# First modulation in blocks of 256 columns, query scores one tile on, and the norms' first roots and second chain in another order

## The chip, the cores and the metric

The kernel runs on one core of a Trainium2 chip. The metric is the device time of one execution in microseconds (us), the median of several runs. A core has TensorE (PE in the rows; its weight loads are PEld), VectorE (DVE), ScalarE (ACT), GpSimd (POOL) and SyncE (SP, which here issues most of the transfers). Each works through a queue of its own in order and waits for the others by semaphores.

## The reference, cut to what is computed

A trunk of two layers over 256 tokens of 1024 columns, in fp32. Layer 0 mixes the tokens with differential attention and a spatial gate, layer 1 with a multi-scale pool; after each mixer stands a PEER layer (product keys, 16 of 16384 experts for each of 8 heads).

```python
for i in range(DEPTH):
    sh1, sc1, g1, sh2, sc2, g2 = jnp.split((silu_c @ ada_w[i] + ada_b[i])[:, None, :], 6, axis=-1)
    hx = modulate(xs, sh1, sc1)                      # xs * (1 + sc1) + sh1
    if ctx_out or even:
        csh1, csc1, cg1, csh2, csc2, cg2 = jnp.split(silu_cc @ ada_w[i] + ada_b[i], 6, axis=-1)
        hc = modulate(cs, csh1, csc1)                # the context, layer 0 alone
    ...
        yx, yc = mixer_ab(hx, hc, ab_w_in[j], ...)   # even; the first product is (hx @ w_in)
    ...
        yx = mixer_pool(hx, pool_w_in[j], ...)       # odd
    xs = layer_norm(alpha * xs + g1 * yx, ln_g[i, 0], ln_b[i, 0])
    hx = modulate(xs, sh2, sc2)
    ...
    fx = peer(hx.reshape(-1, d), peer_wq[i], peer_keys[i], peer_u[i], peer_v[i])
    xs = layer_norm(alpha * xs + g2 * fx, ln_g[i, 1], ln_b[i, 1])
```

What the change touches are the first `modulate` (shift and scale come from 2048 columns of `ada_w[0]`, for the tokens and for the context), the `layer_norm` ahead of each `peer`, the one between the two layers, and the beginning of `peer`: the queries (`hx @ wq`), their scores against the keys, and the search for the best 16.

## The kernel before, in words

**Weights.** All large weights come as tiles of 128 x 1024, in the order in which they are used. A list of items is written out by hand and run in order; every engine's queue holds what the code issues, in that order. For each tile ScalarE copies a rounded high half `hi` (L64), and VectorE, or in the PEER stages GpSimd, makes the low half `lo` by subtraction (L68). A product is three products of halves: high by high, high by low, low by high. `ahead` splits tiles up to three ahead of their use.

**Around a tile.** `item(src, run, after)` is a tile, its products and what is done behind them. `defer(f)` puts `f` off until the products of the next item are issued; nested, it puts it off by as many tiles. `work(budget)` issues a share of the background steps in `bg` (VectorE's searches for the best 16, and the routing that follows) behind each tile. What stands behind a waiting instruction on the same queue waits too.

**Start.** Sixteen adaptive tiles (eight for the shift, eight for the scale) are multiplied by the silu of the two conditions into rows of two partitions (products at L156 to L158, `adrow` copied at L545), turned into columns (L562), added to the bias (L563), and the scale is incremented (L550). `modulated(q)` then makes four blocks of 256 tokens of the input in the two halves: ScalarE with an activation for the high half (L582), VectorE (for `q` of 0) or GpSimd with a multiplication (L584), VectorE the low half by subtraction (L585); `q` of 2 and 3 is the context. The first four tiles of `w_in` are the gate's (`natural`, L610), the next four the gate's input (`transposed`, L616), followed by others and by attention.

**Norms.** Tokens stand in two blocks of 128. `half(nb, c)` is called as each half (512 columns) of a block's output is summed; `norm_part` adds the residual and makes the statistics (up to the variance, L236), `norm_end(nb)` the reciprocal root (L180 to L196, small VectorE instructions; `n_nm` at L251) and the normalised block (L254 on ScalarE, L256 on VectorE), `to_hT` transposes it (L273), scales it (L278, L281) and makes the two halves (L285, L287, L290; the put-off low halves at L943). `mixed` does so ahead of PEER, `second_start` between the layers. In the latter the next stage's first three weight tiles are multiplied block by block: `rowsum_product(..., early=True)` issues 18 products for the first block, in the order of parts 0, 2, 1 (high by high, high of h by low of w, low of h by high of w), and `settle_block` the second block's transposes.

**PEER.** Behind two tiles of keys and 16 tiles of `wq` come 128 tiles of `uT`. Two tiles make one head's query (`query`, L161 and L162), `score` its scores (L156 to L158, copied at L1005), and the searches go into `bg` (L1013 on). `routed` puts the softmax of the routing and the decoding in; the routing's results are transposed at L1093 and L1097. Products with `h` are L984, L985 and L988.

```python
        self.norm_part(nb, c)
        if (nb, c) == (1, 0):
            for _ in self.norm_end(0):
                pass
...
                if j % 2:
                    h = j // 2
                    query(h, st["p"])
                    self.defer(lambda: self.defer(lambda: score(h)))
```

## Time and profile before

| | |
|---|---|
| runs | 2037.8, 2038.82, 2040.18 us |
| median | 2038.82 us |
| profiled execution | 2038.5 us, of which the span is 2036.7 us |
| mean granted clock of TensorE | 0.986 of full speed |
| TensorE busy | 1965.6 us (97%) |
| VectorE busy | 1558.0 us (76%) |
| ScalarE busy | 969.6 us (48%) |
| GpSimd busy | 289.9 us (14%) |
| transfers | 389.93 MB, mean 191 GB/s |

The times of an engine's busy work are sums over the span; what an engine waits for is read from the views of waits and of the timeline. In a timeline each row has its start and its duration in us, the engine, the line of the kernel, the operation, output and inputs by name, and the count of instructions that the row sums; in brackets at its end the idle time before it and what ended that. A matmul's row is longer than its share of the pipeline, since the next starts before it ends: the distance between starts is what it costs.

### The profile page before, as it was taken

Reading aid. Unit: us, or ns where it says so; the run is one execution under the profiler, and the core shown is the slowest. Engines: PE = TensorE matmul, PEld = TensorE weight load, DVE = VectorE, ACT = ScalarE, POOL = GpSimd, SP = SyncE. Lnnn points to the kernel's source line nnn. Section 1 sums busy time; section 2 is a strip of 40 time slices with the busy share of each in tenths; the row PEclk is TensorE's granted clock in tenths of the full one; section 3 lists DMA queues with packets and bytes.
Section 4 is the critical chain, followed back from the end, with each engine's and each line's share of the span. In section 5 each row is a group of like instructions: output and inputs, shape, how many; then the busy total and the mean of one; then the engine's idle time right before and its main releaser. Section 6 shows DMA issues by size and latency. Waiting matters only on the chain.

```text
span 2036.7 us, 34041 instructions
## 1 busy us (share of the span) xinstructions
PE 1965.6 (97%) x13348; PEld 1771.4 (87%) x13348; DVE 1558.0 (76%) x2775; ACT 969.6 (48%) x1354; POOL 289.9 (14%) x134
## 2 busy tenths in 40 slices
PE   8899989999999999999999889999999999999997
PEld 4889869999999998888778779999999998888886
DVE  6878878998888757777776679998888655555566
ACT  6444554544544444444445554445544444444442
POOL 0100007891000000000000016890000000000001
PEclk9899999999999999999999989999999999999999
DMA  8534335554444558888877445554444556555663
GB/s 305 216 135 159 132 116 174 177 176 165 157 148 150 170 185 285 291 305 293 288 263 223 144 161 161 182 176 165 156 146 147 177 180 198 191 195 195 219 236 113
DMA packets 108178, 389.93 MB, mean 191 GB/s; under 512 B 12777, under 2 KB 12905, under 8 KB 108017
## 3 DMA queue, kind: packets, MB, share of 16 engines
q1 hardware_dynamic: 105416, 382.28, 55.8%
q10 hardware_dynamic: 2024, 3.38, 0.5%
q8 instruction: 104, 1.70, 0.3%
q0 software_dynamic: 576, 2.10, 0.3%
q14 instruction: 58, 0.47, 0.1%
HBM read 384.55 MB, written 3.16 MB: 190 GB/s over the span
## 4 chain that ended last, share of the span: by engine, by line
PE 66%; DVE 25%; ACT 4%; issue 3%; DMA 2%; ACTq 0%; SPq 0%; DVEq 0%
PE pa L323 26%; PE px L323 8%; PE pa L984 8%; PE pa L985 7%; PE pa L988 7%; PE pt L1136 2%; DVE lo L68 2%; ACT hi L64 2%; PE pa L616 1%; DVE oh L1063 1%; DVE oh L1068 1%; DVE topi L1014 1%; DVE sc L1015 1%; DVE topi L1017 1%; PE pa L870 1%
## 5 line engine op out<-in xcount | busy, mean ns | idle before, releaser
L64 ACT ACTIVATE hi<-raw 128x1024 fp32r<-128x1024 f32 x599 | 632.6, 1059 | 581.5 <-PE px L323 357.0
L68 DVE TENSOR_TENSOR lo<-raw,hi 128x1024 fp32r<-128x1024 f32 x491 | 599.5, 1224 | 368.8 <-ACT hi L64 366.8
L984 PE MATMUL pa<-h,hi 128*128 128x256 f32 x2304 | 577.9, 288 | 1.5 <-DVE h L287 1.3
L985 PE MATMUL pa<-h,hi 128*128 128x256 f32 x2304 | 566.2, 283 | 0.3
L323 PE MATMUL pa<-hi,h 128*128 128x512 f32 x1524 | 471.7, 391 | 3.3 <-ACT h L285 1.6
L984 PEld LDWEIGHTS pa<-h,hi 128*128 128x128 f32 x2304 | 441.8, 192 | 2.5 <-DVE h L287 2.1
L985 PEld LDWEIGHTS pa<-h,hi 128*128 128x128 f32 x2304 | 442.6, 192 | 0.9 <-DVE h L290 0.9
L323 PEld LDWEIGHTS pa<-hi,h 128*128 128x128 f32 x1524 | 286.3, 188 | 65.9 <-ACT h L285 1.8
L988 PE MATMUL pa<-h,lo 128*128 128x256 f32 x2304 | 323.4, 283 | 0.0
L988 PEld LDWEIGHTS pa<-h,lo 128*128 128x128 f32 x2304 | 297.7, 192 | 0.0
L68 POOL TENSOR_TENSOR lo<-raw,hi 128x1024 fp32r<-128x1024 f32 x106 | 271.0, 2575 | 81.9 <-ACT hi L64 81.6
L323 PE MATMUL pa<-lo,h 128*128 128x512 f32 x762 | 256.5, 391 | 0.1
L323 PE MATMUL px<-hi,h 128*128 128x512 f32 x508 | 197.5, 389 | 0.0
L323 PEld LDWEIGHTS pa<-lo,h 128*128 128x128 f32 x762 | 143.8, 189 | 30.6 <-DVE lo L68 0.5
L1150 ACT ACTIVATE A<-pt 128x256 f32<-128x256 f32 (+31 forms) x182 | 50.9, 310 | 229.1 <-DVE A L1148 215.9
L949 POOL DMA_DIRECT2D xhd<-xh x4 | 2.4, 596 | 960.0 <-PE pt L273 949.8
L323 PEld LDWEIGHTS px<-hi,h 128*128 128x128 f32 x508 | 95.3, 188 | 19.8
L1127 DVE TENSOR_TENSOR m<-e,gd 128x512 f16<-128x512 f16 x256 | 105.4, 454 | 2.2
L323 PE MATMUL px<-lo,h 128*128 128x512 f32 x254 | 98.8, 389 | 0.0
L259 POOL TENSOR_TENSOR aw<-aw 128x512 f32<-128x512 f32 x4 | 5.3, 1344 | 644.6 <-ACT aw L254 644.4
L393 DVE SCALAR_TENSOR_TENSOR aacc<-aw,csil,aacc 128x1024 f32<-128x1024 f32 x70 | 89.5, 1279 | 3.5 <-DMA aw<-in_ada_w 3.4
L1136 PE MATMUL pt<-m,e 128*128 128x128 f16 x1024 | 81.7, 220 | 3.2 <-DVE m L1127 1.0
(365 smaller groups left out, 2151.7 us busy)
## 6 DMA issues: line engine op xcount, KB each, us to landing
raw<-in_uT SPq DMA_DIRECT2D x256, 512.0 KB, 3.5
raw<-in_peer_v SPq DMA_DIRECT2D x256, 512.0 KB, 4.1
aw<-in_ada_w SPq DMA_DIRECT2D x80, 512.0 KB, 5.3
raw<-in_w_in SPq DMA_DIRECT2D x32, 512.0 KB, 4.1
raw<-in_wq SPq DMA_DIRECT2D x32, 512.0 KB, 3.8
raw<-in_ab_w_out SPq DMA_DIRECT2D x12, 512.0 KB, 3.5
raw<-in_ada_w SPq DMA_DIRECT2D x8, 512.0 KB, 5.9
xraw<-in_ada_w SPq DMA_DIRECT2D x8, 512.0 KB
```

Source lines behind the costliest of these rows:

```text
L64: nc.scalar.activation(hi, it["raw"], AF.Copy)
L68: low()
L323: nc.tensor.matmul(acc[2 * nb + a // 512], s[x], w[:, a:b], start=i == 0 and part == 0, stop=i == last and part == 2)
L393: nc.vector.scalar_tensor_tensor(st["acc"], w, c, st["acc"], op0=OP.mult, op1=OP.add)
L616: nc.tensor.matmul(o, (hi, lo)[x][:, 128 * k:128 * k + 128], f(k)[y], start=k == 0 and part == 0, stop=k == 7 and part == 2)
L870: nc.tensor.matmul(p, h(k, s)[x], tiles[k // 4][y][:, 256 * (k % 4):256 * (k % 4) + 256], start=part == 0 and k == 0, stop=part == 2 and k ...
L984: mm(out, hi[:, cs], hh, start=k == 0, stop=False)
L985: mm(out, hi[:, cs], hl, start=False, stop=False)
L988: mm(out, lo[:, cs], self.h(k)[0], start=False, stop=k == 7)
L1127: nc.vector.tensor_tensor(v4(x), v4(st["e1"][:, s]), wide(st["gd"][i], ch, 4), op=OP.mult)
L1136: nc.tensor.matmul(p[:, 128 * j:128 * j + 128], e2[:, j], m[i][:, j], start=i == 0, stop=i == 1)
L1150: nc.scalar.activation(x[:, e:], y[:, e:], AF.Copy, scale=1.0 / 4096)
```

## The change

**Start.** The adaptive columns are laid out anew on the host (`ada01`): four quarters of four tiles, each tile holding two row blocks of 256 shift and 256 scale columns. `quarter(c)` multiplies one quarter's four tiles, copies a row of 512, and, one or two tiles later, turns it into columns and modulates two blocks of 256 tokens. The quarters 1, 2 and 3 stand between the gate tiles in the list of items. The multiplications for the tokens are all VectorE's now (into a tile `xmod`). The context's modulation, `modulated_ctx`, has both its activations on ScalarE; before, GpSimd made the multiplications for three of the four input halves. The context is loaded behind the fourth gate tile in place of the second. **Norms.** `norm_end(0)` stands behind the first block's second half, (0, 1), in place of the second block's first half, (1, 0), in both norms. Between the layers the first block's low halves (`rest`) stand behind the second block's `norm_end`, and `settle_block` stands ahead of part 1 of the first block's products, so behind 12 of the 18. **Query.** `score(h)` is put off by one more tile, and `routed` is called after `uT` tile 2 in place of 1.

```diff
@@ -332,9 +332,10 @@
                     tail.append(x)
                     if i == EARLY - 1:
                         for part in (0, 2, 1):
+                            if part == 1:
+                                self.settle_block()
                             for x in tail:
                                 product(*x, 0, parts=(part,))
-                        self.settle_block()
                         for part in (0, 2, 1):
                             for x in tail:
                                 product(*x, 1, parts=(part,))
@@ -530,59 +531,66 @@
         self.hook(start)
-        for j in range(2):
...
-        def columns_of(j, row):
+        def quarter(c):
+            for kk in range(4):
+                def run(hi, lo, kk=kk):
+                    if kk == 0:
+                        st["ad"] = self.px() if c % 2 else self.pa()
+                    for i in range(2):
+                        k, cs = 2 * kk + i, slice(512 * i, 512 * i + 512)
+                        self.mm3(st["ad"][0:2], (self.cparts[0][:, k], self.cparts[1][:, k]), (hi[:, cs], lo[:, cs]), k == 0, k == 7)
+                    if kk < 3:
+                        return
+                    row = st["G"].tile([2, 512], FT, name="adrow", bufs=2)
+                    nc.scalar.activation(row, st["ad"][0:2], AF.Copy)
+
+                    def turned():
+                        columns_of(c, row)
+                        modulated(c)
+                    if c == 3:
+                        self.defer(turned)
+                    else:
+                        self.defer(lambda: self.defer(turned))
+                self.item(a["ada01"][c, kk], run, after=(lambda: inputs(0, [c])) if kk == 1 and c < 2 else None,
+                          own=(lambda: st["E"]) if kk % 2 else None, owned=2, early=kk % 2)
+
+        def columns_of(c, row):
             p = self.pt()
-            for b in range(8):
+            for b in range(4):
                 nc.tensor.transpose(p[:, 2 * b:2 * b + 2], row[:, 128 * b:128 * b + 128], self.ident[0:2, 0:2])
-            nc.vector.tensor_add(st["cc"][:, j], p[:, :16].rearrange("p (k o) -> p k o", o=2),
-                                 self.adabc[:, 0, j][:, :, None].to_broadcast([128, 8, 2]))
-
-
-        self.holds += 1
+            ks = slice(2 * c, 2 * c + 2)
+            for j in range(2):
+                nc.vector.tensor_add(st["cc"][:, j, ks], p[:, 4 * j:4 * j + 4].rearrange("p (k o) -> p k o", o=2),
+                                     self.adabc[:, 0, j, ks][:, :, None].to_broadcast([128, 2, 2]))
+            nc.vector.tensor_scalar(st["cc"][:, 1, ks], st["cc"][:, 1, ks], 1.0, None, op0=OP.add)
...
-        def modulated(q):
-            if q == 0:
+        def modulated(c):
+            if c == 0:
                 self.hhi, self.hlo = self.htiles()
-            x, y = st["in"][q], st["in"][q | 2]
-            hi = self.hhi[q] if q < 2 else st["hc"][q - 2]
-            lo = self.hlo[q] if q < 2 else st["hc"][q]
-            for k in range(4):
-                kk, o = 4 * (q % 2) + k, q // 2
-                sc, sh = st["cc"][:, 1, kk, o:o + 1], st["cc"][:, 0, kk, o:o + 1]
-                nc.scalar.activation(hi[:, k], x[:, k], AF.Identity, scale=sc, bias=sh)
-                eng = nc.gpsimd if q else nc.vector
-                eng.tensor_scalar(y[:, k], x[:, k], sc, sh, op0=OP.mult, op1=OP.add)
-            nc.vector.tensor_sub(lo, y, hi.bitcast(FT))
+            q, ks = c // 2, slice(2 * (c % 2), 2 * (c % 2) + 2)
+            x, hi, lo = st["in"][q], self.hhi[q], self.hlo[q]
+            y = st["G"].tile([128, 2, 256], FT, name="xmod", bufs=1)
+            for k in range(2):
+                i, kk = 2 * (c % 2) + k, 2 * c + k
+                sc, sh = st["cc"][:, 1, kk, 0:1], st["cc"][:, 0, kk, 0:1]
+                nc.scalar.activation(hi[:, i], x[:, i], AF.Identity, scale=sc, bias=sh)
+                nc.vector.tensor_scalar(y[:, k], x[:, i], sc, sh, op0=OP.mult, op1=OP.add)
+            nc.vector.tensor_sub(lo[:, ks], y, hi[:, ks].bitcast(FT))
+        def modulated_ctx(q):
+            x, hi, lo = st["in"][2 + q], st["hc"][q], st["hc"][2 + q]
+            for i in range(4):
+                kk = 4 * q + i
+                sc, sh = st["cc"][:, 1, kk, 1:2], st["cc"][:, 0, kk, 1:2]
+                nc.scalar.activation(hi[:, i], x[:, i], AF.Identity, scale=sc, bias=sh)
+                nc.scalar.activation(x[:, i], x[:, i], AF.Identity, scale=sc, bias=sh)
+            nc.vector.tensor_sub(lo, x, hi.bitcast(FT))
...
@@ -619,7 +627,11 @@
         w = a["w_in"]
         n = 0
 
+        quarter(0)
         for t in range(4):
+            if t < 3:
+                quarter(t + 1)
+
             def run(hi, lo, t=t):
                 if t == 0:
                     st["gv"] = [self.pa(), self.pa()]
@@ -654,8 +666,8 @@
                         if nb == 0:
                             self.defer(lambda: affine(1))
                     self.defer(lambda: self.defer(lambda: self.defer(stats)))
-            self.item(w[n], run, after=[lambda: small_loads("sgu_ln_g"), lambda: inputs(1), lambda: small_loads("sgu_ln_b"),
-                                         lambda: small_loads("rope")][t])
+            self.item(w[n], run, after=[lambda: small_loads("sgu_ln_g"), lambda: small_loads("sgu_ln_b"),
+                                         lambda: small_loads("rope"), lambda: inputs(1)][t])
             n += 1
 
         def spatial(nb):
@@ -685,7 +697,7 @@
                 if t == 3:
                     lams()
                 if t in (1, 2):
-                    modulated(t + 1)
+                    modulated_ctx(t - 1)
                 if t == 3:
                     pe.close()
                     others()
@@ -927,9 +939,10 @@
             st["full"] = [L.tile([128, 4, 256], FT, name=f"hfull{i}") for i in range(2)]
             self.norm(acc, st["res"], st["grow"], t, x)
         self.norm_part(nb, c)
-        if (nb, c) == (1, 0):
+        if (nb, c) == (0, 1):
             for _ in self.norm_end(0):
                 pass
+        if (nb, c) == (1, 0):
             self.lows = []
         if (nb, c) != (1, 1):
             return
@@ -1171,7 +1184,7 @@
                 if j % 2:
                     h = j // 2
                     query(h, st["p"])
-                    self.defer(lambda: self.defer(lambda: score(h)))
+                    self.defer(lambda: self.defer(lambda: self.defer(lambda: score(h))))
             self.item(a["wq"][l, j], run, after=after, budget=2.4, lo="v" if j < 3 else "g")
 
         def opened():
@@ -1221,7 +1234,7 @@
                     evacuate(t - 1, st["pp"])
 
             def after(t=t):
-                if t == 1:
+                if t == 2:
                     routed()
                 if len(st["A"]) == 2:
                     gate_step()
@@ -1305,7 +1318,7 @@
         if (nb, c) == (0, 0):
             self.norm(acc, xa, row, ts, ts)
         self.norm_part(nb, c)
-        if (nb, c) == (1, 0):
+        if (nb, c) == (0, 1):
             for _ in self.norm_end(0):
                 pass
         if (nb, c) != (1, 1):
@@ -1315,9 +1328,12 @@
         st["px"] = ExitStack()
         P = st["L"] = st["px"].enter_context(tc.tile_pool(name="second", bufs=1))
         full = [V.tile([128, 4, 256], FT, name="aw", bufs=3) for i in range(2)]
-        self.to_hT(0, *st["hs"], full)
+        rest = []
+        self.to_hT(0, *st["hs"], full, rest)
         for _ in self.norm_end(1):
             pass
+        for f in rest:
+            f()
         self.settle_block = lambda: self.second_rest(st, ts, full, pools)
 
     def second_rest(self, st, ts, full, pools):
@@ -1453,6 +1469,8 @@
     a = dict(x=g["x"][0], ada_w=g["ada_w"], ada_b=g["ada_b"], ln_g=g["ln_g"], ln_b=g["ln_b"])
     for n, x in (("xT", "x"), ("cT", "ctx")):
         a[n] = g[x][0].T.reshape(2, 4, 128, 256).transpose(0, 2, 1, 3).reshape(2, 128, 1024)
+
+    a["ada01"] = g["ada_w"][0][:, :2048].reshape(4, 2, 128, 2, 4, 256).transpose(4, 0, 2, 1, 3, 5).reshape(4, 4, 128, 1024)
     a["cc"] = np.stack([g["c"][0].reshape(8, 128).T, g["c_ctx"].reshape(8, 128).T], axis=2)
     a["ada_bc"] = cols(g["ada_b"].reshape(2, 6, 1024))
     a["ln_gc"], a["ln_bc"] = cols(g["ln_g"]), cols(g["ln_b"])
```

How the queues change is shown at three places, all on VectorE. The first is at the start of the program, from the seventh pair of adaptive low halves on (`lo`, `xlo`: low halves of weight tiles; `mod`: the columns; `h`: the input's low half). Before:

```order
L68 TENSOR_TENSOR lo<-raw,hi 128x1024
L563 TENSOR_TENSOR mod_127<-pt,adabc 128x16
L68 TENSOR_TENSOR xlo<-xraw,xhi 128x1024
L68 TENSOR_TENSOR lo<-raw,hi 128x1024
L68 TENSOR_TENSOR xlo<-xraw,xhi 128x1024
L563 TENSOR_TENSOR mod_127<-pt,adabc 128x16
L550 TENSOR_SCALAR mod_127<-mod_127 128x16
L68 TENSOR_TENSOR lo<-raw,hi 128x1024
L584 TENSOR_SCALAR in_136<-in_134,mod_127 128x256 x4
L585 TENSOR_TENSOR h<-in_136,h 128x1024
L68 TENSOR_TENSOR lo<-raw,hi 128x1024
L585 TENSOR_TENSOR h<-in_137,h 128x1024
```

Of the change, from the ninth low half on:

```order
L68 TENSOR_TENSOR lo<-raw,hi 128x1024
L563 TENSOR_TENSOR mod_127<-pt,adabc 128x4 x2
L565 TENSOR_SCALAR mod_127<-mod_127 128x4
L582 TENSOR_SCALAR xmod<-in_134,mod_127 128x256 x2
L583 TENSOR_TENSOR h<-xmod,h 128x512
L68 TENSOR_TENSOR lo<-raw,hi 128x1024
L68 TENSOR_TENSOR xlo<-xraw,xhi 128x1024
L68 TENSOR_TENSOR lo<-raw,hi 128x1024
L563 TENSOR_TENSOR mod_127<-pt,adabc 128x4 x2
L565 TENSOR_SCALAR mod_127<-mod_127 128x4
L582 TENSOR_SCALAR xmod<-in_134,mod_127 128x256 x2
L583 TENSOR_TENSOR h<-xmod,h 128x512
```

The first modulation moved from behind all adaptive low halves to behind the ninth, and came in four sets of two additions, one increment, two multiplications and one subtraction; 3, 5 and 4 low halves stand between a set and the next.

The second place is the norm between the layers, from the second block's variance on (`n_ve`; `rs_` names are the root's). Before:

```order
L236 TENSOR_SCALAR n_ve<-n_mv 128x1
L290 TENSOR_TENSOR h<-aw,h 128x4x128 x2
L180 TENSOR_SCALAR rs_y<-n_ve 128x1
L183 SCALAR_TENSOR_TENSOR rs_r<-rs_y,n_ve 128x1
...
L251 SCALAR_TENSOR_TENSOR n_nm<-n_mv,rs_y 128x1
L256 TENSOR_SCALAR aacc<-aacc,n_mv,rs_y 128x512
L281 TENSOR_SCALAR aw<-pt,hs_11754,hb_11755 128x128 x4
L287 CAST h<-aw 128x4x128
```

Of the change:

```order
L236 TENSOR_SCALAR n_ve<-n_mv 128x1
L180 TENSOR_SCALAR rs_y<-n_ve 128x1
L183 SCALAR_TENSOR_TENSOR rs_r<-rs_y,n_ve 128x1
...
L251 SCALAR_TENSOR_TENSOR n_nm<-n_mv,rs_y 128x1
L256 TENSOR_SCALAR aacc<-aacc,n_mv,rs_y 128x512
L1336 TENSOR_TENSOR h<-aw,h 128x4x128 x2
L281 TENSOR_SCALAR aw<-pt,hs_11770,hb_11771 128x128 x4
L287 CAST h<-aw 128x4x128
```

The first block's two subtractions for the low halves (`h<-aw,h`) moved from ahead of the second block's root to behind its normalising.

The third place is the beginning of PEER, where the first search starts (`topv<-sc`). Before:

```order
L162 TENSOR_TENSOR keys_3154<-raw,keys_3153 128x1024
L162 TENSOR_TENSOR q_3188<-pa,q_3187 128x512
L162 TENSOR_TENSOR keys_3154<-raw,keys_3153 128x1024
L1013 MAX topv<-sc 128x8
L1014 MAX_INDEX topi<-topv,sc 128x8
...
L1017 MAX_INDEX topi<-px,sc 128x8
L162 TENSOR_TENSOR q_3280<-pa,q_3279 128x512
```

Of the change:

```order
L162 TENSOR_TENSOR keys_3173<-raw,keys_3172 128x1024
L162 TENSOR_TENSOR q_3207<-pa,q_3206 128x512
L162 TENSOR_TENSOR keys_3173<-raw,keys_3172 128x1024
L162 TENSOR_TENSOR q_3289<-pa,q_3288 128x512
L1026 MAX topv<-sc 128x8
L1027 MAX_INDEX topi<-topv,sc 128x8
```

The second query's low half moved ahead of the first search. On TensorE the first score stands behind four `wq` tiles in place of three, and the routing's transposes behind 51 weight tiles of PEER in place of 50, in both layers.

## Rows read from the trace of the kernel before

**Rows 1.** The page's first part: busy us, share of the span, instructions.

```profile
PE 1965.6 (97%) x13348; PEld 1771.4 (87%) x13348; DVE 1558.0 (76%) x2775; ACT 969.6 (48%) x1354; POOL 289.9 (14%) x134
```

**Rows 2.** Waits of TensorE: us in total, times, longest.

```profile
PE pt L158 <- DVE q L162: 5.3, 12, 0.6
PE pt L1097 <- DVE best L1086: 2.8, 2, 1.4
```

**Rows 3.** Timeline of TensorE, 24 to 60 us: start, us, instruction, count.

```profile
38.76 4.54 PE L610 MATMUL pa<-hi,h 128*128 128x512 f32 x12 [1.02 <-DVE h L585]
...
46.78 1.98 PE L610 MATMUL pa<-hi,h 128*128 128x512 f32 x8
...
49.50 2.08 PE L616 MATMUL pa<-h,hi 128*128 128x256 f32 x16
```

**Rows 4.** Timeline of ScalarE and VectorE, first 45 us.

```profile
17.14 1.23 DVE L68 TENSOR_TENSOR lo<-raw,hi 128x1024 fp32r<-128x1024 f32 x1
...
19.73 0.59 ACT L545 ACTIVATE adrow<-pa 2x512 f32<-2x512 f32 x1
...
35.09 2.28 DVE L584 TENSOR_SCALAR in<-in,mod 128x256 f32<-128x256 f32 x4
...
36.78 2.06 ACT L582 ACTIVATE h<-in,mod 128x256 fp32r<-128x256 f32 x4
...
40.87 1.06 ACT L64 ACTIVATE hi<-raw 128x1024 fp32r<-128x1024 f32 x1 [1.08 <-PE pa L610]
...
40.89 2.35 DVE L68 TENSOR_TENSOR lo<-raw,hi 128x1024 fp32r<-128x1024 f32 x2
```

**Rows 5.** Timeline of TensorE, 57 to 67 us.

```profile
66.32 0.74 PE L616 MATMUL pa<-hc,hi 128*128 128x256 f32 x4 [0.83 <-DVE hc L585]
```

**Rows 6.** One-us windows of TensorE: stretch, us, busy, granted clock, DMA share, GB/s.

```profile
39.00:40.00 1.00, 1.00 (x3) 0.50 0.00 0
```

**Rows 7.** Timeline, 277 to 305 us: the norm ahead of the first PEER.

```profile
281.66 0.15 DVE L236 TENSOR_SCALAR n_ve<-n_mv 128x1 f32<-128x1 f32 x1
...
285.31 0.16 DVE L251 SCALAR_TENSOR_TENSOR n_nm<-n_mv,rs_y 128x1 f32<-128x1 f32 x1
...
292.11 0.69 DVE L943 TENSOR_TENSOR h<-hfull,h 128x512 fp32r<-128x512 f32 x1 [0.60 <-ACT h L285]
...
294.60 0.58 PE L984 MATMUL pa<-h,hi 128*128 128x256 f32 x1 [0.65 <-DVE h L287]
```

**Rows 8.** Timeline, 1112 to 1150 us: the norm between the layers.

```profile
1124.95 0.15 DVE L236 TENSOR_SCALAR n_ve<-n_mv 128x1 f32<-128x1 f32 x1
...
1126.34 0.15 DVE L180 TENSOR_SCALAR rs_y<-n_ve 128x1 int32<-128x1 int32 x1
...
1128.05 0.16 DVE L251 SCALAR_TENSOR_TENSOR n_nm<-n_mv,rs_y 128x1 f32<-128x1 f32 x1
...
1131.14 0.15 DVE L236 TENSOR_SCALAR n_ve<-n_mv 128x1 f32<-128x1 f32 x1
...
1132.03 2.93 PE L323 MATMUL pa<-hi,h 128*128 128x512 f32 x6 [1.55 <-ACT h L285]
...
1134.67 0.15 DVE L180 TENSOR_SCALAR rs_y<-n_ve 128x1 int32<-128x1 int32 x1
...
1138.90 1.03 PE L273 MATMUL pt<-ident,aacc 128*128 128x128 f32 x8
...
1141.43 0.50 PE L323 MATMUL pa<-hi,h 128*128 128x512 f32 x1 [1.49 <-DVE h L287]
```

**Rows 9.** Timelines of the first query stage, engine by engine, 296 to 475 us.

```profile
309.38 0.58 ACT L1005 ACTIVATE sc<-pt 128x512 f32<-128x512 f32 x1
...
309.50 2.59 DVE L162 TENSOR_TENSOR keys<-raw,keys 128x1024 fp32r<-128x1024 f32 x1 [3.53 <-ACT keys L161]
...
430.80 29.40 POOL L68 TENSOR_TENSOR lo<-raw,hi 128x1024 fp32r<-128x1024 f32 x10 [0.29 <-ACT hi L64]
...
458.01 0.44 PE L1097 MATMUL pt<-ident,best 128*128 128x128 f32 x2 [1.39 <-DVE best L1086]
```

More of the change, by code (lines that the diff above doesn't have):

```diff
@@ L530, in first @@
         self.hook(start)
-        for j in range(2):
-            for k in range(8):
-                def run(hi, lo, j=j, k=k):
-                    if k == 0:
-                        st["ad"] = [self.pa(), self.px()]
-                    for c in range(2):
-                        cs = slice(512 * c, 512 * c + 512)
-                        self.mm3(st["ad"][c][0:2], (self.cparts[0][:, k], self.cparts[1][:, k]), (hi[:, cs], lo[:, cs]),
-                                 k == 0, k == 7)
-                    if k == 7:
-                        row = st["G"].tile([2, 1024], FT, name="adrow", bufs=1)
-                        for c in range(2):
-                            nc.scalar.activation(row[:, 512 * c:512 * c + 512], st["ad"][c][0:2], AF.Copy)
-                        if j == 0:
-                            self.defer(lambda: self.defer(lambda: self.defer(lambda: columns_of(0, row))))
-                        else:
-                            columns_of(1, row)
-                            nc.vector.tensor_scalar(st["cc"][:, 1], st["cc"][:, 1], 1.0, None, op0=OP.add)
-                            self.release(1)
-                            modulated(0)
-                            self.ahead(self.now, 1)
-                            modulated(1)
-                self.item(a["ada_w"][0, 128 * k:128 * k + 128, 1024 * j:1024 * j + 1024], run,
-                          after=(lambda q=k: inputs(0, [q])) if (j, k) in ((1, 0), (1, 1)) else None,
-                          own=(lambda: st["E"]) if k % 2 else None, owned=2, early=k % 2)
```

## Prediction

> **What bounds the kernel now.** The page's first part comes first: TensorE is busy for 97% of the span [rows 1], so time can be won only where it waits, or where its clock is down. The view of waits says where that is; of its rows the two that the query edit touches are shown [rows 2]. The timeline was then read at four places. (a) The first 50 us: the gate product (twelve products for each of four weight tiles, 2.72 a tile at full rate: from 46.78 to 49.50, so 0.23 each) waits and crawls while the modulated input comes, and the next product starts at 49.50 [rows 3]. (b) The norm before each PEER layer. (c) The norm between the two layers. (d) The query stage. The reader is to see in each who is waited for: in (a) ScalarE and VectorE, in (b) and (c) a chain of small VectorE instructions, in (d) a VectorE that has no gap left.
>
> **The change, part by part.**
>
> *Start.* The 16 adaptive tiles stay 16, and their 96 products and 16 low halves too; new are four row copies and four times (two additions, one increment, two multiplications, one subtraction on VectorE; two activations on ScalarE) in place of two and two larger sets. What moves is when each of these stands in the queues. I walk the new order with old durations: a low half follows the one before by 1.18 (two in 2.35), a copy takes 1.06, an activation of 256 columns 0.52 (four in 2.06), a multiplication 0.57 (four in 2.28), a row copy 0.59, a small addition 0.2 (0.15 and a gap) [rows 4, 7]. VectorE reaches the first quarter's additions behind nine low halves. The ninth started at 17.14 [rows 4] and ended at 18.3; the row copy that now stands ahead of the eighth weight's copy makes that 18.9. Each quarter then costs the two engines in turn 0.6 (additions), 1.1 (activations; the multiplications lie beside them), 1.05 (the next weight's copy, which stands behind the activations; the subtraction lies beside it), so 2.75, and the low halves that stand before the next quarter's additions: 3, 5 and 4 of them, 14.2. That is 18.9 + 3 x 2.75 + 14.2 = 41.3 for the last low half ahead of the fourth quarter, and 43.0 for that quarter's activations. TensorE meanwhile takes the last quarter's row copy (behind a copy that ends about 1.2 before 41.3, so 40.7), 0.5 of transposes, and two gate tiles of 2.72: 46.6. With a few tenths for handovers I take 47.0, against 49.50: **2.5 gained**. Bounds: nothing, if each of the three full cycles costs 0.9 more than these rows; and 3.9, if ScalarE never holds VectorE up (the same VectorE work without gaps, 18.9 + 12 x 1.18 + 4 x 2.45 = 42.9, and one tile behind it, 45.6). The 16 context activations (8 before, and 12 GpSimd multiplications besides) add 8 x 0.52 = 4.2 to ScalarE; they lie beside the gate-input products, where ScalarE has gaps. Before, TensorE waited 0.83 there for the context half that GpSimd had made late [rows 5]; were ScalarE just as late as it gains here, the 2.5 would be gone. The context loads are queued behind two more weight loads (the seven that follow stand ahead of them on SyncE's queue); their user comes after two more gate-input tiles, about 5 us on, so I charge nothing; if they were late, the context activations and the copies queued behind them would be.
>
> Whether the gain survives the next stage: there TensorE waits for VectorE's low halves (L870), and VectorE's chain starts from the same products, so it starts earlier by the same amount. I keep the 2.5 whole.
>
> The clock belongs to this term. Before, TensorE's granted clock was down at its lower level, 0.50, amid these waits (the stretch from 39 to 40), and twelve gate products took 4.54 instead of 2.72 [rows 3, 6]. In my walk the longest wait is near 1.5, so I take the full rate. The Trainium skill speaks against that: "TensorE: Matmul & The Clock Gate", section "HAM oscillation — how this bites in real kernels", says that a loop whose bursts of products are short against the waits between them can find the clock down at every burst. By that rule the interleaving would be slower, as in the third rival; the trace so far agrees with it only for the stretch of rows 6.
>
> *Norms before PEER (twice).* The first block's root chain (ten small instructions) is issued as soon as its variance is there: after 281.66 instead of behind the second block's first half, where it ended at 285.31 [rows 7], so about 1.7 sooner. The second block's statistics still wait for the last product, so its chain doesn't move. What does move is ScalarE's part for the first block: VectorE's wait of 0.60 for it at 292.11 goes, and with it the first PEER product's start at 294.60, which hangs on that VectorE queue [rows 7]. **0.6 each**; bounds 0 and 1.0 (that and the half of its 0.65 wait).
>
> *Norm between the layers.* First block: its root started at 1126.34 although the variance was made at 1124.95 (0.15 long): 1.2 sooner, and so is the first pool product, at 1132.03 [rows 8]. Second block: its variance is made at 1131.14, but its root started at 1134.67, behind the first block's low halves; these are put off, so it starts near 1131.3, and its transposes go ahead of the last six of the eighteen products. In numbers, at the low clock that the rows show: first product 1130.8; twelve products in 5.7 (six took 2.93; 24 x 0.23 would be 5.5), 1136.5; transposes 1.03, 1137.5; the last six, with the clock coming back, until about 1139.3. VectorE's scaling and cast lie beside them: the next product started 2.5 behind the start of the transposes (1138.90 to 1141.43), so now at 1139.0 at the earliest. 1139.3 against 1141.43 [rows 8]: **2.1 gained**. If the shorter waits leave the clock up, the twelve take 2.8, and the second block's chain sets the start: root and normalising 2.4 (by the first block's 1.8, 1126.34 to 1128.2, and a pass that I put at 0.6), 1133.7, two put-off subtractions of 0.69 [rows 7], 1135.1, scaling and cast 1.9 (the 2.5 less four transposes), 1137.0: 4.4. Lower bound 1.2, the first block's alone.
>
> *Query scores one tile on (twice).* TensorE waited for the low half of the query 5.3 in all, and 2.8 at the routing's transposes, for VectorE's last gate instruction [rows 2]. Between them VectorE shows no wait: it runs on from 312.1, when the second key tile's low half (309.50, 2.59 long) ends, to the gates whose transposes start at 458.01 [rows 9]. So it isn't enough to take the 5.3 away: the time at which the routing can be transposed is VectorE's. What counts is (i) whether VectorE starts later, and (ii) how much TensorE has done by then. (i) What held the first search up was the key tile: the first score's copy had started at 309.38 [rows 9]. It now stands behind one more weight copy, so near 311.0 to 311.6, still before 312.1. The second query's low half (0.69) goes ahead of the search, which so starts near 312.8 with that 0.69 already done. No change. (ii) By the new order 51 weight tiles stand ahead of the routing's transposes, not 50. A tile takes 2.9 (GpSimd, which keeps step with it, did ten in 29.40 [rows 9]). There is enough waiting to give it: per layer 5.3/2 + 2.8/2 = 4.0. **2.9 each.** Bounds: 0, if the search starts a whole tile later after all, and 4.0.
>
> *Sum.* 2.5 + 2 x 0.6 + 2.1 + 2 x 2.9 = 11.6. The profiled execution's own time is 2038.5 (span 2036.7, 1.8 around it), so 2026.9; the median of the runs is 0.3 higher than it, so **2027.2**. A measurement of this kernel can tell about 0.2% (4.1 us) from no change.
>
> **The rivals.** *The query wait only changes its place.* VectorE's work between first score and routing is fixed; if its start moves on by the tile too, TensorE's 5.3 is given back at the routing's transposes (1.39 then grows by some 2.9), and the two 2.9 are lost: 2033.0. For it: no gap on VectorE. Against it: the search waits for the keys, not for the score. Chance 0.15.
>
> *The start gives nothing.* The four handovers cost 0.9 more each than their rows: 2029.7. For it: an in-order ScalarE that waits for columns holds the next copies. Chance 0.17.
>
> *Slower: the clock in the first 50 us.* If the granted clock falls at the first quarter's wait (near 20 us) and stays at its lower level, eleven adaptive tiles of 6 products (0.23 apart at full rate, 1.4 a tile) and four gate tiles take twice as long: 11 x 1.4 + 4 x 2.72 = 26 more, of which the waits swallow about 3. Then 2027.2 + 23 = 2050.2. It decides from about half of that stretch at the lower level: 11.6 of extra time eats the whole gain. Against it: waits in the walk are under 1.5. Chance 0.04.
>
> *More than forecast.* The clock stays up in the norm between the layers (2.3 more), the start runs gap-free (1.4), VectorE's earlier start in the norms carries to the routing (0.4 each): 2022.7. Chance 0.16. The forecast itself: 0.48.
>
> **How the numbers follow.** The upper end lies above the query rival's 2033.0, since the start may give less at the same time: 2034.5. The lower end takes in the last case and a little of the 4.0 bound: 2020.5. Faster by over 0.2% means under 2034.7: all cases but the clock one and the part of the query case in which another term fails too, 0.89; within 0.2%: 0.07; slower 0.04.
>
> **What would show it.** Right: the product after the gate tiles starts near 47 with the clock at its upper level from 11 on; the wait for the query's low half nearly gone in the first heads, VectorE's search starting no later against the first PEER product, the routing's wait still 1 to 2 us, with one more tile ahead of it; the first product of the second block between the layers about 2 us sooner against the end of the product before. Wrong: a routing wait of 4 us or more; ScalarE waiting over 2 us at each quarter; a granted clock of 0.50 between 18 and 47; TensorE waiting several us for the context half.

## The result and the profile after

| | before | after |
|---|---|---|
| median of the runs | 2038.31 us (4 runs) | 2024.91 us (2024.42 to 2026.39, 4 runs) |
| span of the profiled execution | 2036.7 us | 2022.9 us |
| mean granted clock | 0.986 | 0.990 |

The ratio is 0.9935, with a 95% interval of 0.9923 to 0.9946: 13.4 us less, where 11.6 were forecast (2027.2, range 2020.5 to 2034.5). A ladder of landmarks in the two traces says where it came from; the last column is the difference to the row above.

| landmark | before | after | sooner | step |
|---|---|---|---|---|
| first gate-input product | 49.50 | 46.47 | 3.0 | 3.0 |
| first block's variance, first norm before PEER | 281.66 | 281.34 | 0.3 | -2.7 |
| first PEER product | 294.60 | 293.39 | 1.2 | 0.9 |
| first product with peer_v | 764.82 | 760.10 | 4.7 | 3.5 |
| first block's variance between the layers | 1124.95 | 1120.19 | 4.8 | 0.0 |
| second block's first product there | 1141.43 | 1132.15 | 9.3 | 4.5 |
| first block's variance, second norm before PEER | 1191.94 | 1182.58 | 9.4 | 0.1 |
| first PEER product | 1204.34 | 1194.64 | 9.7 | 0.3 |
| first product with peer_v | 1675.22 | 1661.42 | 13.8 | 4.1 |
| end of the span | 2036.7 | 2022.9 | 13.8 | 0.0 |

The page's first part, after:

```profile
PE 1958.0 (97%) x13348; PEld 1767.1 (87%) x13348; DVE 1551.9 (77%) x2790; ACT 974.3 (48%) x1358; POOL 281.4 (14%) x122
```

TensorE's waits, after (us in total, times, longest). The row of the score's products on the query [rows 2] is gone; the routing's is as it was, now with one tile more ahead of it. The low halves of the v products and the second block's normalised half are still the longest waits behind the start.

```profile
PE pa L882 <- DVE lo L68: 12.8, 4, 4.5
PE pt L273 <- DVE xh L256: 8.9, 2, 4.7
...
PE pt L1110 <- DVE best L1099: 2.9, 2, 1.5
```

The start, after: timelines of VectorE (the last quarter's additions), of TensorE, and one window of TensorE. The gate products start at 40.89 and 43.75, 2.72 to 2.86 apart, where twelve of them took 4.54 before [rows 3].

```profile
41.38 0.22 DVE L563 TENSOR_TENSOR mod<-pt,adabc 128x4 f32<-128x4 f32 x2
```

```profile
43.75 1.98 PE L618 MATMUL pa<-hi,h 128*128 128x512 f32 x8
...
46.47 2.08 PE L624 MATMUL pa<-h,hi 128*128 128x256 f32 x16
...
58.92 2.18 PE L624 MATMUL pa<-h,hi 128*128 128x256 f32 x16 [0.78 <-ACT hi L64]
...
64.70 0.74 PE L624 MATMUL pa<-hc,hi 128*128 128x256 f32 x4 [1.04 <-DVE hc L593]
```

```profile
24.00:28.00 4.00, 3.26 (x18) 1.00 1.03 410
```

The first norm before PEER, after (timeline): the root's chain ends 1.90 behind the variance, 3.65 in [rows 7], VectorE's put-off low halves wait for nothing, and the first PEER product comes 12.05 behind the variance, 12.94 before.

```profile
281.34 0.15 DVE L236 TENSOR_SCALAR n_ve<-n_mv 128x1 f32<-128x1 f32 x1
...
283.24 0.16 DVE L251 SCALAR_TENSOR_TENSOR n_nm<-n_mv,rs_y 128x1 f32<-128x1 f32 x1
...
290.31 1.29 DVE L956 TENSOR_TENSOR h<-hfull,h 128x512 fp32r<-128x512 f32 x2
...
293.39 0.58 PE L997 MATMUL pa<-h,hi 128*128 128x256 f32 x1 [1.61 <-DVE h L287]
```

The norm between the layers, after (timeline): the root follows the variance in both blocks, and the first block's first six products take 1.67, not the 2.93 of [rows 8] at the lower clock.

```profile
1120.19 0.15 DVE L236 TENSOR_SCALAR n_ve<-n_mv 128x1 f32<-128x1 f32 x1
1120.38 0.15 DVE L180 TENSOR_SCALAR rs_y<-n_ve 128x1 int32<-128x1 int32 x1
...
1126.07 1.67 PE L323 MATMUL pa<-hi,h 128*128 128x512 f32 x6 [1.55 <-ACT h L285]
...
1126.82 0.15 DVE L180 TENSOR_SCALAR rs_y<-n_ve 128x1 int32<-128x1 int32 x1
...
1132.15 0.50 PE L323 MATMUL pa<-hi,h 128*128 128x512 f32 x1 [0.45 <-DVE h L287]
```

The query stage, after (timelines of VectorE and TensorE): the search starts 17.25 behind the first PEER product, 17.41 before, and the transposes wait 1.39, as in [rows 9].

```profile
310.64 0.28 DVE L1026 MAX8 topv<-sc 128x8 f32<-128x128 f32 x1
```

```profile
455.36 0.44 PE L1110 MATMUL pt<-ident,best 128*128 128x128 f32 x2 [1.39 <-DVE best L1099]
```

### The profile page after: what moved, and what is told of

Read it like the earlier page. It is cut to its first block, busy times and chain, and to the rows that moved or that the text cites. A ratio compares the mean times of both kernels' runs of the same rounds, so it can differ in the third digit from the quotient of the medians.

```text
span 2022.9 us, 34054 instructions
## 1 busy us (share of the span) xinstructions
PE 1958.0 (97%) x13348; PEld 1767.1 (87%) x13348; DVE 1551.9 (77%) x2790; ACT 974.3 (48%) x1358; POOL 281.4 (14%) x122
## 4 chain that ended last, share of the span: by engine, by line
PE 69%; DVE 23%; DMA 3%; issue 2%; ACT 2%; ACTq 0%; SPq 0%; DVEq 0%
PE pa L323 27%; PE pa L997 9%; PE px L323 9%; PE pa L1001 8%; PE pa L998 8%; PE pt L1149 3%; PE pa L624 2%; DVE lo L68 1%; DVE oh L1076 1%; DVE oh L1081 1%; DVE topi L1027 1%; DVE sc L1028 1%; DVE topi L1030 1%; PE pa L882 1%; DVE idx L1082 1%
## 5 line engine op out<-in xcount | busy, mean ns | idle before, releaser
L1163 ACT ACTIVATE A<-pt 128x256 f32<-128x256 f32 (+21 forms) x180 | 50.2, 309 | 230.8 <-DVE A L1161 224.4
L1140 DVE TENSOR_TENSOR m<-e,gd 128x512 f16<-128x512 f16 x256 | 101.0, 436 | 2.2
```

Source lines behind the costliest of these rows:

```text
L1140: nc.vector.tensor_tensor(v4(x), v4(st["e1"][:, s]), wide(st["gd"][i], ch, 4), op=OP.mult)
L1163: nc.scalar.activation(x[:, e:], y[:, e:], AF.Copy, scale=1.0 / 4096)
```

## The experiments

Each kernel is the change with the edit shown, if nothing else is said. Ratios are to the kernel before, measured beside it; the change itself has 0.9935 (0.9923 to 0.9946). A difference to the change is one of medians, if nothing else is said. The kernel before had 2038.1 beside 1, 4, 7 and 8, 2039.2 beside 2, 3, 6 and 9, and 2037.6 beside 5, 10, 11 and 12, so differences by ratios come out up to 1.7 apart from those of medians. From their intervals, the difference of two ratios is uncertain by some 3.5 us (an estimate): 4, 5, 6 and 12 differ clearly from the change, 7 and 9 just, and 1, 3, 8, 10 and 11 can't be told from it by their runs alone.

**1. The start undone.** `quarter`, `modulated` and `modulated_ctx` are replaced by the code of before.

> The change with its first modulation as it was before (sixteen adaptive tiles, one modulation behind them, GpSimd's share of the context), all else of the change kept. Theory A (the ladder of the two traces: the start's 3.0 us are given back by the norm ahead of the first PEER, where only 0.3 is left): the time rises by 0 to 1 us, about 2025.5; gate-input products start near 49.5 again, the first block's variance of the first norm at most 0.5 later than with the change. Rival (the prediction: the gain is kept whole): 2.5 to 3.0 more, 2027.4 to 2028.

Measured: 2027.17 us, ratio 0.9948 (0.9935 to 0.9962), 2.3 more than the change, 2.6 by the ratios. The gate-input products started at 49.93, the first norm's variance at 282.45, 1.1 later than in the change's trace; at the second layer's first peer_v product 0.6 was left. By the runs that is nearer the rival, by the trace nearer theory A.

**2. The start alone**, on the kernel before.

> The kernel before with the new start alone (quarters, VectorE's multiplications, the context on ScalarE); norms and query as before. Theory A (four traces with the new start reach the first norm's variance 1.0 us sooner than the two with the old one, though their gate-input products start 3.4 sooner): 0.6 to 1.6 less than before, about 2037.2. Rival (the prediction, 2.5 kept whole): 2035.6 or less. Second rival (nothing left at all): 2038.3.

Measured: 2035.86, ratio 0.9982 (0.9973 to 0.9991), 3.7 less than before by the ratio. In its trace the variance comes at 280.46, 1.2 sooner than before, and 1.5 are left at the second layer's first peer_v product. Over all profiles, the gate-input product starts at 46.0 in the mean of eleven with the new start (all but experiment 3) and at 49.7 in two with the old; the variance at 280.65 and 282.06. So of 3.7 us, 1.4 reach the norm. The runs say 2.6 and 3.7, uncertain by some 3.5 and 1.8 to either side; whether 1.4 or 2.5 is right stays open.

**3. A load moved ahead**, to see what swallows the start's gain.

```diff
-  self.ada(P, 0, j, ...)
+  self.ada(P, 0, j, ..., ahead=2 if j == 2 else 1)
```

> The change with the first of the adaptive vectors that VectorE sums during attention loaded two tiles ahead instead of one, so that its second multiplication doesn't wait for its tile. Theory A (what swallows the start's gain is VectorE's wait of 3.9 us at 78.0 for that tile, behind which the low halves stand for which TensorE waits 4.5 and 3.6): the waits of the v products for low halves fall from 12.8 to 5 to 9 and the time by 2 to 4 us, about 2022. Rival (VectorE's other work in that stretch takes the same time anyway, or the tile is late from another transfer): within 1 us of the change.

Measured: 2026.73, ratio 0.9940 (0.9927 to 0.9954): no gain. The v products' waits for low halves fell from 12.8 to 9.0, as theory A has it, and the v products with the context started at 90.90 instead of 97.35, 6.4 sooner (timelines of TensorE, this kernel, then the change), but the first norm's variance came at 280.39, as in the other profiles.

```profile
90.90 2.07 PE L882 MATMUL pa<-hi,hc 128*128 128x256 f32 x16
```

```profile
97.35 2.08 PE L882 MATMUL pa<-hi,hc 128*128 128x256 f32 x16
```

The windows of TensorE (stretch, us, busy, clock, DMA share, GB/s) show where most of it went, in the same order.

```profile
200.00:220.00 20.00, 16.21 (x107) 0.84 0.35 107
```

```profile
200.00:220.00 20.00, 20.00 (x167) 1.00 0.45 158
```

Attention gives back even a lead of 6.4. In that stretch TensorE waits 1.55, 0.21 and 2.02 for high and low halves of later v tiles, and its clock is down for a part. What sets the end of this stage was not isolated.

**4. The query edit undone.**

```diff
-  self.defer(lambda: self.defer(lambda: self.defer(lambda: score(h))))
+  self.defer(lambda: self.defer(lambda: score(h)))
-  if t == 2: routed()
+  if t == 1: routed()
```

> The change with scores put off by two tiles and the routing after tile 1, as before; all else kept. Theory A (the waits cost TensorE more than their rows say: the ladder gives 4.3 us a layer up to the routing's transposes, of which 0.8 and 0.2 are given back later): 7 to 8.5 us more, about 2032.5. Rival (the prediction's term, one tile of 2.9 a layer): 5.8 more, 2030.7. Either way the wait of the score's products for the query's low half comes back, 5.3 us by its rows, and 50 tiles stand ahead of the routing's transposes.

Measured: 2031.11, ratio 0.9967 (0.9955 to 0.9979), 6.2 more than the change. From the first PEER product to the first peer_v product it takes 3.0 and 2.9 more in the two layers. The prediction's size is right; of the ladder's 3.5 and 4.1, 0.1 and 0.4 come with the norms' edit (experiment 10), and the rest of the difference wasn't assigned.

**5. The tile ahead of the routing without the score's move**: the edit of 4, and

```diff
-  self.bg.append((14.0, lambda: None))
+  self.bg.append((16.4, lambda: None))
```

> The change with scores put off by two tiles and the routing appended after tile 1, as before, but the routing's transposes one tile later by the delay alone (14.0 raised to 16.4): 51 tiles ahead of them, as in the change. Theory A (what the query edit gave is the tile ahead of the routing, since VectorE sets that time): 2025 to 2027, as fast as the change within 2 us, though the waits for the query's low half, 5.3 by their rows, are back. Rival (what it gave is the removal of those waits): 2031, as with the whole query edit undone; TensorE then reaches the transposes a tile later, with VectorE waiting for it.

Measured: 2033.04, ratio 0.9971 (0.9959 to 0.9983), no faster than 4: the rival's side. With 51 tiles ahead of the routing the wait at its transposes is gone, VectorE now waited 1.3 for TensorE, and the first maps came late (waits of TensorE in this kernel):

```profile
PE pt L158 <- DVE q L162: 4.4, 11, 0.6
PE pt L1149 <- DVE m L1140: 3.5, 4, 1.6
```

VectorE waits the same 1.3 in experiment 6, where a tile ahead does gain, so TensorE's lateness alone doesn't explain the loss. The two kernels part behind the transposes. Here a comparison of VectorE lies beside one more subtraction of GpSimd and takes 2.89; in experiment 6 GpSimd has no weight left to split by then, and it takes 0.69. From the transposes to the first map product it is 10.6 here and 8.9 there. Timelines of VectorE and GpSimd in this kernel, then of VectorE in experiment 6's:

```profile
463.50 2.89 DVE L1134 TENSOR_TENSOR e<-iota,i2d 128x1024 f16<-128x1024 f16 x1
```

```profile
463.31 2.53 POOL L68 TENSOR_TENSOR lo<-raw,hi 128x1024 fp32r<-128x1024 f32 x1 [0.47 <-ACT hi L64]
```

```profile
462.41 0.69 DVE L1134 TENSOR_TENSOR e<-iota,i2d 128x1024 f16<-128x1024 f16 x1
```

So the tile without the score's move gained nothing. What the score's move gives without the tile, no run shows.

**6. One tile more ahead of the routing, scores as in the change**: the edit of 5 on the change alone.

> The change with the routing's transposes one weight tile later again (a delay in the list of VectorE's background steps raised from 14.0 to 16.4), scores as in the change; 52 tiles ahead of the transposes. Theory A (VectorE alone sets when the routing is ready, TensorE has no other wait in this stage, so a tile put ahead fills the 1.4 us that it waits): the wait of 1.39 goes and the time falls by 1.0 to 2.8 us, about 2023. Rival (VectorE's work behind the transposes, the one-hots and maps, starts later by what TensorE now takes, and sets the rest of the uT stage): no change, 2024.5 to 2025.5; the map products then run later and the waits behind the routing grow by as much.

Measured: 2019.13, ratio 0.9898 (0.9882 to 0.9913), 5.8 less than the change (7.5 by the ratios), more than theory A's 2.8. The transposes start without a wait, VectorE waits 1.3 for them (timeline of VectorE, this kernel):

```profile
455.82 0.69 DVE L1107 CAST i1d<-pt 128x512 f16<-128x512 f32 x1 [1.32 <-PE pt L1106]
```

The first map product comes only 0.8 later behind the first PEER product (at 292.50 here, 293.39 in the change), though a tile of 2.9 more lies ahead of it, and it no longer waits. The timelines of TensorE, first of this kernel, then of the change:

```profile
464.68 0.62 PE L1149 MATMUL pt<-m,e 128*128 128x128 f16 x8
```

```profile
464.78 0.89 PE L1149 MATMUL pt<-m,e 128*128 128x128 f16 x8 [0.35 <-DVE m L1140]
```

Between the first PEER and the first peer_v product it is 2.9 and 2.0 less. 1.4 and 1.5 of it are the wait at the transposes; the rest stands around the first maps and had not been foreseen.

**7. The first block's root late again, between the layers alone.**

```diff
-  if (nb, c) == (0, 1):    # in second_start
+  if (nb, c) == (1, 0):
```

> The change with only the first block's root between the layers back at its old place (behind the second block's first half); the put-off low halves and the earlier second block are kept. Theory A (the clock fell before because of the wait of 2.55 us ahead of the first block's transposes, and the change's shorter wait of 1.31 kept it up): the wait is 2.3 to 2.6 again, the granted clock falls to 0.50 within the first block's 18 products, which take about twice 4.1 us; 3 to 4 us more, about 2028.5. Rival (the clock has another cause, say the second wait, which the change kept short): the clock stays at 1.00 and the time rises by 1.2 at most, to 2026.1.

Measured: 2028.57, ratio 0.9957 (0.9943 to 0.9970), 3.7 more (4.5 by the ratios). The wait was 2.33, the clock fell to its lower level behind it, and from the first block's variance to the second block's second product (on `px`, 0.3 behind the one of the ladder) passed 14.9 instead of 12.3. A window of TensorE in this kernel:

```profile
1124.00:1126.00 2.00, 1.58 (x8) 0.50 0.00 0
```

That fits theory A, but other runs take away its certainty: in five kernels that keep the change's norm between the layers (3, 5, 6, 9 and 10) the clock fell too, behind a first wait of 1.2 or less and a second of 1.6, where the change itself had waited 1.31 and 1.55 and kept it. TensorE's windows in experiment 3's kernel, and in the change's:

```profile
1126.00:1128.00 2.00, 2.00 (x5) 0.50 0.00 0
```

```profile
1127.00:1129.00 2.00, 2.00 (x10) 1.00 0.00 0
```

The same distance was 12.3 where the clock stayed at 1.00 (the change, 1, 4 and 8), 14.4 in 3 and 13.2 in 5, 6, 9 and 10; before it was 16.8 with the clock down. So much the same waits left the clock at either level, and the norm's edits are worth 2.4 to 4.5 accordingly.

**8. The second block's wait before PEER filled** (outputs of the added transposes are unused).

```diff
+  def fill(self, n):
+      p = self.pt()
+      for k in range(n):
+          c = 128 * (k % 4)
+          self.nc.tensor.transpose(p[:, c:c + 128], self.ident, self.ident)
...
+  self.fill(24)            # in mixed's settle_block
   self.to_hT(1, hs, hb, st["full"])
```

> The change with 24 transposes of the identity (output unused) on TensorE ahead of the second block's transposes in both norms before PEER, where it waits 4.2 and 4.7 us. Theory A (VectorE sets the time of the routing's transposes): the clock stays at 1.00, the first PEER tile takes 2.9 instead of 5.0, but TensorE only reaches the routing's transposes sooner and waits there 1.4 us more or so: the time falls by 0 to 1 us a layer, 2023 to 2025. Rival (TensorE's own work sets it, and the clock's 2.2 us are pure loss): 2.0 to 2.5 less a layer, 2020 to 2021. If the transposes don't hold the clock up, or are late themselves, the time stays or rises by up to 1.

Measured: 2025.15, ratio 0.9936 (0.9922 to 0.9949): no change. Waits of 1.6 and 1.8 were left, and the clock fell behind them all the same, to 0.51 in 294 to 296. It doesn't tell the theories apart.

**9. Both waits of that norm filled**: `self.fill(32)` ahead of the transposes and `self.fill(12)` behind them.

> The change with 32 transposes of the identity ahead of the second block's transposes in both norms before PEER, and 12 behind them (output unused). Theory A (with both waits filled the clock stays at 1.00 through the first PEER tile, but the weight tiles that follow land no sooner and VectorE sets the routing): first tile 2.9 instead of 4.1 to 5.2, the third tile waits for its high half 1 to 2 us, time unchanged within 1 us, 2024 to 2025.5. Rival (the low clock costs its 2 us in full, twice): 2020.5 to 2021.5. The filler itself may be late by some tenths.

Measured: 2022.54, ratio 0.9916 (0.9902 to 0.9929), 2.4 less (3.9 by the ratios). The clock stayed up (window of TensorE, this kernel, then the change):

```profile
294.00:296.00 2.00, 2.00 (x19) 1.00 0.17 25
```

```profile
294.00:296.00 2.00, 1.89 (x9) 0.50 0.03 8
```

To the first peer_v product it is 0.9 and 1.0 less in the two layers. The wait at the routing stayed, at 1.4 and 1.6, so VectorE was sooner by as much as TensorE: neither theory had that.

**10. The first root late again in the norms before PEER**: in `mixed`, `norm_end(0)` at (1, 0).

> The change with the first block's root back behind the second block's first half in the two norms before PEER; all else kept. Theory A (the prediction's 0.6 each; the two traces show 0.9 and 0.3): 1.2 more, 2026.1; the distance from the first block's variance to the first PEER product 12.9 again instead of 12.05. Rival (the low halves and the key tiles behind it wait for transfers anyway, and VectorE sets the routing): no change, 2024.9.

Measured: 2026.49, ratio 0.9943 (0.9929 to 0.9957), 1.6 more, which the runs alone don't tell from none. From the first block's variance to the first PEER product it is 12.94 and 12.40 again, 12.05 and 12.06 in the change: 0.9 and 0.3 by the traces, as predicted in sum.

**11. The waits between the layers filled**: `self.fill(8)` ahead of the first block's transposes, `self.fill(12)` behind them.

> The change with 8 and 12 transposes of the identity (output unused) in TensorE's two waits between the layers, ahead of the first block's transposes and ahead of its first product. Theory A (the same short waits left the clock at 1.00 in five profiles and at 0.50 in three, so the waits decide it only together with what went before; filled, it stays at 1.00 always): clock 1.00, 2024.9 as in the change's own profile, with runs that differ less. Rival (the clock's fall there has nothing to do with these waits): 0.50 in about every third run, or the transposes cost what they take, up to 0.5.

Measured: 2024.00, ratio 0.9927 (0.9914 to 0.9941), not to be told from the change. The clock was 1.00 and the distance 12.3, as it was in the change's own profile. One profile can't show that it always stays up. (Of the unfilled profiles that the expectation counts, four had kept the clock, not five: the change, 1, 4 and 8.)

**12. Edits 6, 9 and 11 together.**

> The change with the routing's transposes one tile later (as in the run with the delay of 16.4) and with transposes of the identity (output unused) in the waits of all three norms: 32 and 12 in the norms before PEER, 8 and 12 between the layers. Theory A (each of the two gave its own: 5.8 and 2.4 us by the runs, and filled waits hold the clock up between the layers in every run): about 2017, the granted clock 1.00 through the first block's 18 products. Rival (filling only brings TensorE sooner to the routing's transposes, where it then waits for VectorE, since the later turn has no wait left to give): 2018.5 to 2020.

Measured: 2015.87, ratio 0.9889 (0.9874 to 0.9904), the fastest of all, 9.0 less than the change (9.4 by the ratios). The distance between the layers is 12.3. It lies below the rival's 2018.5 and meets theory A; against 6 alone the intervals overlap.

## Why the prediction was right

**The start.** The end of the walk holds: the last quarter's additions came at 41.38 (forecast 41.3), its row copy at 39.92 (40.7), the gate-input product at 46.47 (46.6, taken as 47.0). In part that is luck. The first quarter's additions came at 20.05, not 18.9, since VectorE waited 1.38 for a copy of ScalarE, which had waited for its weights; then each cycle took 2.54 instead of 2.75, and a low half 1.14 or 1.15 instead of 1.18, which made up for it (timeline of VectorE, after):

```profile
17.67 1.23 DVE L68 TENSOR_TENSOR xlo<-xraw,xhi 128x1024 fp32r<-128x1024 f32 x1 [1.38 <-ACT xhi L64]
...
20.05 0.23 DVE L563 TENSOR_TENSOR mod<-pt,adabc 128x4 f32<-128x4 f32 x2
```

The clock stayed at 1.00 from 11 to 48, so the slower rival did not come, with waits of 0.6 and 0.7 between the bursts of products. The step that failed is the one behind it, that the gain is kept whole: the context cost 0.78 and 1.04 of waits where 0.83 stood before [rows 5], since ScalarE's eight activations a half hold the weight copy, and then the second half's subtraction. Behind it 1.6 of the 3.0 are left (timelines of TensorE, before, then after), and attention took most of the rest.

```profile
66.89 1.12 PE L616 MATMUL pa<-hc,lo 128*128 128x256 f32 x8
```

```profile
65.28 1.12 PE L624 MATMUL pa<-hc,lo 128*128 128x256 f32 x8
```

Of 3.0 in the two traces 0.3 was left at the first norm, of 3.7 in the mean of all 1.4; the runs allow 2.5. The prediction's reading of the 0.83 was not exact either: in the trace of before, VectorE has no gap ahead of that subtraction at 65.05, so it was its own queue that was late there.

**Norms before PEER.** 0.9 and 0.3 for 0.6 each. As forecast, what is left is the second block's chain, for which TensorE waits 4.2 and 4.7.

**Norm between the layers.** 4.5 for 2.1. The mechanism was as told, and both sizes were near: 4.4 had been worked out for a clock that stays up, and at the low clock the experiments gave 2.4 to 3.6. The choice between them was wrong for this execution, and it isn't one that the kernel makes alike each time.

**Query.** 5.9 by the traces and 6.2 by the runs when it is undone, for 5.8. Of the reason, one half was wrong and the other is open. Wrong is that VectorE's time stays where it is. Its last gate instruction ends 161.9 and 162.0 behind the first PEER product in the two kernels with the later scores (the change and 6), and 162.9 and 163.1 in the two with the earlier ones (4 and 5): the score's move brought it 1.0 forward. The rows of the change and of 4, whose first PEER products start at 293.39 and 293.44:

```profile
453.40 1.90 DVE L1099 TENSOR_TENSOR best<-best,gsm 128x256 f32<-128x256 f32 x1
```

```profile
454.39 1.91 DVE L1099 TENSOR_TENSOR best<-best,gsm 128x256 f32<-128x256 f32 x1
```

With the tile of 2.9 that makes 3.8 at the transposes, of which 3.0 are left at the end of the stage: the size is right partly because these two errors, of 1.0 and 0.9, cancel. Open is what the tile is worth by itself. Without the score's move it gained nothing (experiment 5); the move without the tile was not run, though by these rows TensorE would then have reached the transposes 2.9 sooner and waited there for VectorE, an estimate that speaks for the prediction's reason.

The rows' 5.3 of waits [rows 2] are less than what the waits cost. Three tiles with two scores among them take 12.48 in experiment 4's kernel and 11.32 in the change; with one score 10.75 and 9.98. Over the first 21 tiles of the first layer that is 4.2, where the rows of that kernel show 2.6; with 0.3 lost in the tile ahead of them it is the 3.8 above. The windows of TensorE show it as a count, first before, then after: in the same 20 us, at a full clock, 155 products against 171, though only 1.31 are idle; 16 products of 0.12 are 1.9.

```profile
320.00:340.00 20.00, 18.69 (x155) 1.00 0.48 155
```

```profile
320.00:340.00 20.00, 20.00 (x171) 1.00 0.51 168
```

Up to the first maps the lead grows to 4.3, and about 1.3 of it is given back behind tile 99: there eight tiles with their maps take 3.7 to 4.0 instead of 3.4 in the change, six in experiment 4's kernel, and the maps end a tile later; by the order the first map stands behind 54 tiles, not 53.

**The sum.** Too high at the start, too low between the layers, the rest right in size: the total is good partly by luck, because these two errors cancel.

## What to carry to other kernels

A gain at the head of a program is worth what is left of it at the next place where another engine or a transfer sets the end: follow it there in the trace before counting it. Count products in a stretch rather than adding idle times: a short wait costs a pipelined engine more than its row says. Where two engines meet at a handover, move work until neither waits, and then try one step on: the best point here was one tile beyond the change. Look at what the step then falls beside: the same tile gained nothing with the scores at their old place.

## What the runs showed of the hardware

VectorE's instructions with two inputs stretched beside GpSimd's subtraction. In the change, a comparison of 128x1024 took 2.89 while GpSimd made a low half, ending 0.55 behind it, and 0.68 a little later, when GpSimd made none; timelines of VectorE and GpSimd:

```profile
459.29 2.89 DVE L1135 TENSOR_TENSOR e<-iota,i1d 128x1024 f16<-128x1024 f16 x1
...
467.62 0.68 DVE L1135 TENSOR_TENSOR e<-iota,i1d 128x1024 f16<-128x1024 f16 x1
```

```profile
458.94 2.69 POOL L68 TENSOR_TENSOR lo<-raw,hi 128x1024 fp32r<-128x1024 f32 x1 [1.38 <-ACT hi L64]
```

The Trainium skill, "SBUF — State Buffer", section "Who interferes with whom", says that a VectorE instruction with two SBUF inputs and a GpSimd instruction that reads SBUF exclude each other for a whole instruction; these rows agree. Experiments 5 and 6 show the same pair, 2.89 and 0.69. It may be why the wait at the routing was 1.4 before, 1.4 and 1.5 after, and 1.4 and 1.6 with filled norms: the instruction waited for (`best`, 128x256, 1.90 us) also stands beside GpSimd's subtractions, whose pace is TensorE's. No run here took GpSimd away, so that link is argued and not shown.

Between the layers TensorE's granted clock stayed at 1.00 (2.4 GHz) or fell to 0.50 (1.2 GHz) behind much the same two waits: it stayed in the change and in 1, 4 and 8, with a first wait of 0.5 to 1.3 and a second of 1.6, and fell in 3, 5, 6, 9 and 10, with a first of 1.2 or less and a second of 1.6. The products and transposes ahead of the waits were the same; no run tells what decides it.
